# An encoder's second channel mixer with its sample tokens as 2x2 block products, seven for eight

## The chip, the cores and the metric

The kernel runs on one core of one Trainium2 chip. The metric is the time of one execution on the device, in microseconds (us). Of every kernel the median of several executions is given, beside one profiled execution that a hardware profiler recorded.

## The reference

A two-layer encoder over 256 prompt tokens and 1024 sample tokens of width 1024. Layer 0 mixes tokens with a recurrence, layer 1 with a neighbourhood attention; a channel mixer follows each. Only the second channel mixer (layer 1, behind the attention) is at stake here:

```python
D_MODEL = 1024; SEQ = 256; DEC_SEQ = 1024; D_FF = 4 * D_MODEL

def _sq_relu_mlp(h, w_up, w_down):
    return jnp.square(jax.nn.relu(h @ w_up)) @ w_down
...
    x = x + y                                # y: the token mixer, its output product (w_no) in it
    x = x + _sq_relu_mlp(_rms_norm(x, p['norm_mlp_g'][layer]), p['w_up'][layer], p['w_down'][layer])
```

All of it is float32.

## The kernel before

Every array lies with its channels over the 128 partitions, eight blocks of channels deep, and its tokens along the free axis. Tokens go in three segments, `SEGS = [(0,256),(256,768),(768,1280)]`: the prompt (s = 0) and two halves of the sample (s = 1, 2). A float32 product is made of three matmuls on a split of both factors into a rounded part (hi) and what is left (lo): hi by hi, hi by lo, lo by hi. That is `mm3`, lines 108 to 110, one matmul on each line, and these lines are the matmuls of the profile's rows. A weight block is loaded (L101, SyncE's queue), rounded by ScalarE (`whi`, L102), and its rest is subtracted by GpSimd, in the `w_no` part by VectorE (`wlo`, L103). Below, a *unit* is one matmul of 128x128 weights with 512 tokens; one with 256 tokens counts half.

`channel_layer(1, x_d, "at_d", "w_no", out)` does layer 1's mixer, all products being plain:

- *Output product of the attention.* For eight row blocks m of `w_no`, segments 0 and 1, then again for segment 2: `dense` (8 x 3 matmuls), VectorE adds the residual (L1433), ScalarE and GpSimd the squares for the norm (L1260, L1261), and `split_x` writes hi and lo of the scaled x into the tiles `act` (ahp/alp, ahs/als; L1268, L1269).
- *Up and down, interleaved.* For each of 32 hidden blocks f: `up(f, s)` multiplies by `w_up`, takes the ReLU on ScalarE (L1459), the square on GpSimd (L1460), hi on ScalarE (L1462) and lo on VectorE (L1463), into SBUF. `down([f - 1], s)` multiplies the hidden block before it by eight blocks of `w_down`, and VectorE adds each result to x in SBUF (L1481).
- *The norm* is not applied ahead of the products: x is multiplied by the mean square `ms` (`scale`, L1443 to L1446), and at the last hidden block the sum is multiplied by its inverse (L1483) and stored.

```python
            for f in range(2, NF - 1):
                for s in range(3):
                    up(f, s)
                    down([f - 1], s)
                ...
                wdown(f)
```

Each engine works through its queue in the order in which its instructions stand there; a scheduler (Tile) fixes that order when the kernel is built, by its own costs, except where the code pins it for TensorE (`manual_schedule`). Between engines there are semaphores: an instruction that waits holds up all that stand behind it on its engine. Tiles come from pools; a tile that takes over the place of another waits until that one's last reader is done.

## Time and profile before

| | |
|---|---|
| median of 3 executions | 4020.34 us (4017.2 to 4024.3) |
| the profiled execution | 4024.14 us, its span 4022.4 us, mean granted TensorE clock 0.969 |
| TensorE busy | 3744.8 us (93% of the span) |
| VectorE, ScalarE, GpSimd busy | 2477.0, 1535.1, 1501.4 us |
| DMA | 387.74 MB, mean 96 GB/s |

How to read the rows shown below: L108 is a line of the kernel; engines are PE (TensorE matmul), PEld (its weight loads), DVE (VectorE), ACT (ScalarE), POOL (GpSimd), SP (SyncE, which issues transfers). A group's row has its line, engine, operation, `out<-in`, the tile's partitions x elements and the count, then busy us in all, mean ns of one, the engine's idle time just ahead of them and what ended it. Busy engines are not by themselves what bounds: matmuls are pipelined, so that a row's 390 ns for one matmul is a latency, and its price is the distance between two of them.

### The profile page before, as it was taken

How to read it: one execution, taken by the hardware profiler on the slowest of the kernel's cores; microseconds unless marked ns; L12 is line 12 of the kernel's file. 1: busy time of each engine (PE TensorE's matmuls, PEld its weight loads, DVE VectorE, ACT ScalarE, POOL GpSimd, SP SyncE). 2: the span in 40 equal slices, each digit the busy share in tenths (PEclk: the TensorE clock that was granted, in tenths of full speed). 3: DMA queues.
4: the chain of work that ended last, by engine and by line, in shares of the span. 5: the costliest groups of instructions: out<-in, count | busy, mean ns of one | idle time of the engine just before them, and what ended most of it. 6: DMA issues, size and time to landing. Idle time of an engine off the chain costs nothing.

```text
span 4022.4 us, 82971 instructions
## 1 busy us (share of the span) xinstructions
PE 3744.8 (93%) x33028; PEld 3104.7 (77%) x33028; DVE 2477.0 (62%) x4691; ACT 1535.1 (38%) x3587; POOL 1501.4 (37%) x1568
## 2 busy tenths in 40 slices
PE   7888989888888799999999989999989999999999
PEld 4665669766667688888888879777758888888887
DVE  7897975577775466555555560666774755555555
ACT  6776763344445331121121142555663221121121
POOL 4451112365666543222222240455552422222222
PEclk8998989899999899999999999999989999999999
DMA  3326666666776421111111135333344111111111
GB/s 107 92 79 233 230 211 184 162 151 163 178 162 173 145 73 37 37 43 37 37 43 37 37 98 168 80 70 83 78 113 135 47 37 37 43 37 37 43 32 63
DMA packets 397428, 387.74 MB, mean 96 GB/s; under 512 B 163792, under 2 KB 318640, under 8 KB 397040
## 3 DMA queue, kind: packets, MB, share of 16 engines
q1 hardware_dynamic: 337328, 292.10, 26.6%
q10 hardware_dynamic: 46704, 61.35, 4.5%
q0 software_dynamic: 13008, 28.99, 2.4%
q8 instruction: 260, 4.26, 0.5%
q14 instruction: 128, 1.05, 0.1%
HBM read 272.30 MB, written 121.24 MB: 98 GB/s over the span
## 4 chain that ended last, share of the span: by engine, by line
PE 62%; DVE 7%; POOL 4%; issue 4%; ACT 3%; DMA 2%; SPq 0%; ACTq 0%; DVEq 0%; POOLq 0%
PE ps L108 17%; PE ps L109 17%; PE ps L110 17%; PE kps L1003 2%; PE op L1934 1%; PE bo L1044 1%; PE ba L1044 1%; PE pt L1876 1%; ACT ll L1013 1%; PE qps L956 1%; PE bu L1044 1%; POOL z_d L1210 1%; DVE zz L1008 1%; PE nst L1671 1%; PE vps L527 1%
## 5 line engine op out<-in xcount | busy, mean ns | idle before, releaser
L1481 DVE TENSOR_TENSOR x<-ps,x 128x256 f32<-128x256 f32 x1488 | 812.5, 594 | 609.4 <-PE ps L110 609.4
L103 POOL TENSOR_TENSOR wlo<-raw,whi 128x1024 fp32r<-128x1024 f32 (+1 forms) x178 | 391.6, 2200 | 849.0 <-ACT whi L102 848.9
L108 PE MATMUL ps<-ahs,whi 128*128 128x512 f32 x1536 | 612.9, 399 | 0.0
L109 PE MATMUL ps<-als,whi 128*128 128x512 f32 x1536 | 599.5, 390 | 0.4 <-POOL als L1367 0.4
L110 PE MATMUL ps<-ahs,wlo 128*128 128x512 f32 x1536 | 599.1, 390 | 0.0
L108 PE MATMUL ps<-hh,whi 128*128 128x512 f32 (+1 forms) x1536 | 545.5, 355 | 12.2 <-DVE x L1481 12.1
L109 PE MATMUL ps<-hl,whi 128*128 128x512 f32 (+1 forms) x1536 | 544.0, 354 | 0.0
L110 PE MATMUL ps<-hh,wlo 128*128 128x512 f32 (+1 forms) x1536 | 543.6, 354 | 0.0
L102 ACT CAST whi<-raw 128x1024 fp32r<-128x1024 f32 (+1 forms) x206 | 201.2, 977 | 688.9 <-PE ps L109 631.7
L1460 POOL TENSOR_TENSOR rl<-rl 128x512 f32<-128x512 f32 (+1 forms) x192 | 174.1, 907 | 490.3 <-PE ps L110 451.0
L108 PEld LDWEIGHTS ps<-ahs,whi 128*128 128x128 f32 x1536 | 288.9, 188 | 62.2 <-issue 6.9
L110 PEld LDWEIGHTS ps<-ahs,wlo 128*128 128x128 f32 x1536 | 288.5, 188 | 61.8
L108 PEld LDWEIGHTS ps<-hh,whi 128*128 128x128 f32 x1536 | 290.0, 189 | 55.8 <-DVE x L1481 15.6
L109 PEld LDWEIGHTS ps<-als,whi 128*128 128x128 f32 x1536 | 288.9, 188 | 54.0 <-issue 1.0
L110 PEld LDWEIGHTS ps<-hh,wlo 128*128 128x128 f32 x1536 | 290.4, 189 | 40.6
L109 PEld LDWEIGHTS ps<-hl,whi 128*128 128x128 f32 x1536 | 290.4, 189 | 40.1
L1459 ACT ACTIVATE rl<-ps 128x512 f32<-128x512 f32 (+1 forms) x192 | 100.7, 524 | 533.2 <-PE ps L110 533.2
L1462 ACT CAST hh<-rl 128x512 fp32r<-128x512 f32 (+1 forms) x192 | 105.5, 550 | 321.4 <-POOL rl L1460 321.3
L108 PE MATMUL ps<-ahp,whi 128*128 128x256 f32 x768 | 222.1, 289 | 0.0
L1008 DVE TENSOR_TENSOR zz<-kps,cst 128x512 f32<-128x512 f32 x160 | 110.7, 692 | 174.6 <-ACT ll L1013 174.4
L110 PE MATMUL ps<-ahp,wlo 128*128 128x256 f32 x768 | 215.3, 280 | 0.7 <-POOL wlo L103 0.7
L109 PE MATMUL ps<-alp,whi 128*128 128x256 f32 x768 | 215.1, 280 | 0.0
(336 smaller groups left out, 8325.9 us busy)
## 6 DMA issues: line engine op xcount, KB each, us to landing
x<-x_d SPq DMA_DIRECT2D x88, 512.0 KB, 6.3
raw<-in_w_down_dram SPq DMA_DIRECT2D x64, 512.0 KB, 3.5
raw<-in_w_up_dram SPq DMA_DIRECT2D x64, 512.0 KB, 3.5
x_d<-ar ACTq DMA_DIRECT2D x32, 512.0 KB, 3.2
x_d<-bk ACTq DMA_DIRECT2D x32, 512.0 KB, 5.3
bs<-tab SPq DMA_DIRECT2D x128, 96.0 KB, 4.3
v_d<-vt ACTq DMA_DIRECT2D x80, 128.0 KB, 3.5
uv<-v_d SPq DMA_DIRECT2D x80, 128.0 KB, 7.4
```

What stands on the lines that cost most here:

```text
L102: nc.scalar.copy(hi[:, cs], raw)
L103: lo_eng.tensor_tensor(out=lo[:, cs], in0=raw, in1=hi[:, cs].bitcast(F32), op=ALU.subtract)
L108: mm(ps, sh, mh, start=first, stop=False)
L109: mm(ps, sh, ml, start=False, stop=False)
L110: mm(ps, sl, mh, start=False, stop=last)
L1003: mm(J["kp"][out, e, 192 * c + 192 - w:192 * c + 192], x[es, b, 2 * pr + c], x[es, 5 - w // 64:5, 2 * pr + c], start=True, stop=True)
L1008: nc.vector.tensor_tensor(out=z, in0=src[:, :, :, :P], in1=self.mask[d].unsqueeze(1).unsqueeze(1).to_broadcast([P, 2, 2, P]), op=ALU.mult)
L1044: mm = lambda out, a, b, start, stop: nc.tensor.matmul(out, a, b, start=start, stop=stop, skip_group_check=True)
L1459: nc.scalar.activation(r[:, :n], ps[:, :n], AF.Relu)
L1460: nc.gpsimd.tensor_tensor(out=r[:, :n], in0=r[:, :n], in1=r[:, :n], op=ALU.mult)
L1462: nc.scalar.copy(hh[:, :n], r[:, :n])
L1481: nc.vector.tensor_tensor(out=xv, in0=ps[:, :n], in1=xv, op=ALU.add)
```

## The change

`run` calls `mixer7(1, x_d, "w_no", out)` in place of `channel_layer(1, ...)`; layer 0 stays with `channel_layer`, and `act_tiles` only gives its tiles names by which their places can be taken over later. The two halves of the sample make the columns of a 2x2 block matrix B, two halves of the inner dimension its rows; two row blocks of the weight by those halves make A. Winograd's form then needs seven products in place of eight (A11B11, A12B21, S1T1, S2T2, S3T3, S4B22, A22T4), with S sums of weight blocks and T sums of B. The prompt's tokens are done plainly, 256 at a time. There are two stages in place of the interleaving:

- *Up*, 16 steps n, each a pair of hidden blocks. The S of step n + 1 are four GpSimd operations (`up_raw`) on the two loaded weight tiles `raws[0]`, `raws[1]` into `raws[2]`, `raws[3]`; each of the four is then split on ScalarE and VectorE (`up_unit`). Two products that are added accumulate in the same PSUM bank, whose value in between ScalarE copies out (`t1`, `t5`). For n below 14 the seven hidden operands of the down stage (B11, B21, B22, T1 to T4 of the hidden blocks) are formed on GpSimd, split, and stored by SP to DRAM (`h_d`, 512 KB each, through a ring of three tiles `ho`), as are the prompt's two (`hp_d`); step 14 stores its four plain blocks, and step 15 keeps them in SBUF (`keep`).
- *Down*, 16 steps. First pair 15, plain, from SBUF: prompts, then `keep[1]` and `keep[2]`, then `keep[0]` and `keep[3]`. Then pairs 0 to 13 with seven products, four times j each (27 units), and pair 14 plain. Their operands come back from DRAM (`fetch`, on GpSimd's queue, into 13 tiles). VectorE adds PSUM to the accumulators `acc`, 128x1024 at a time, 16 times a step. `down_sums` (GpSimd, 4 x 128x512) and `chunk` (16 casts on ScalarE, 16 subtracts of 128x256 on GpSimd a step) prepare the weights of the next step. The residual, stored to DRAM in the output product (`xn_d`), is loaded, scaled and added by GpSimd over steps 2 to 13; `combine(j)`, 7 GpSimd operations each, makes the four output blocks of the seven sums in step 14, and the last step adds pair 14, scales and stores.

```diff
...
-            return [[pool.tile([P, n], F32R, name=f"{x}{part}{k}") for x in ("ah", "al")] for k in range(KT)]
+            return [[pool.tile([P, n], F32R, name=f"{x}{part}{k}", tag=f"{x}{part}{k}") for x in ("ah", "al")] for k in range(KT)]
...
+    def mixer7(self, layer, x_src, wname, dst):
...
+        xn_d = self.dram("xn_d", [8, P, T])
+        h_d = self.dram("h_d", [NP - 1, 7, P, 2, 512])
+        hp_d = self.dram("hp_d", [NP - 1, 2, P, 2, TP])
...
+        def cut(x, hi, lo, eng):
+            nc.scalar.copy(hi, x)
+            sub(eng, lo, x, hi.bitcast(F32))
...
+            raws = [wr.tile([P, 1024], F32, name="raw", tag=f"raw{i}") for i in range(4)]
...
+            def up_raw(n):
+                r, q = raws[:2], raws[2:]
+                for i in range(2):
+                    nc.sync.dma_start(r[i], a["w_up"][layer, 2 * n + i])
+                add(nc.gpsimd, h0(q[0]), h0(r[1]), h1(r[1]))
+                sub(nc.gpsimd, h1(q[0]), h0(r[0]), h0(r[1]))
+                sub(nc.gpsimd, h0(q[1]), h0(q[0]), h0(r[0]))
+                sub(nc.gpsimd, h1(q[1]), h1(r[0]), h0(q[1]))
...
+            def up_prep(i, n):
+                if i == 0:
+                    up_raw(n)
+                    up_unit(raws[0], ("A11", "A12"))
+                elif i == 1:
+                    up_unit(raws[3], ("S2", "S4"))
+                elif i == 2:
+                    up_unit(raws[2], ("S1", "S3"))
+                else:
+                    up_unit(raws[1], ("A21", "A22"))
...
+            def give(n, i, t):
+                if n == NP - 1:
+                    cut(t, *keep[i], nc.vector)
+                    return
+                o = out_tile()
+                cut(t, o[:, 0], o[:, 1], nc.vector)
+                nc.sync.dma_start(h_d[n, i], o.bitcast(F32))
...
+                for n in range(NP):
+                    nxt = lambda i: up_prep(i, n + 1) if n < NP - 1 else None
+                    plain = n >= NP - 2
+                    b1 = bank()
+                    product(b1, "A11", "B11", True, False)
+                    t1 = tmp("p")
+                    nc.scalar.copy(t1, b1)
+                    ps = bank()
+                    prompt(ps, 0)
+                    give_prompt(n, 0, ps)
+                    product(b1, "A12", "B21", False, True)
+                    h11 = tmp("h")
+                    relu2(h11, b1)
+                    nxt(0)
+                    b6 = bank()
+                    product(b6, "S2", "T2")
+                    add(nc.vector, t1, b6, t1)
+                    give(n, 0, h11)
+                    b5 = bank()
+                    product(b5, "S1", "T1", True, False)
+                    t5 = tmp("q")
+                    nc.scalar.copy(t5, b5)
+                    ps = bank()
+                    prompt(ps, 1)
+                    give_prompt(n, 1, ps)
+                    product(b5, "S4", "B22", False, True)
+                    h12 = tmp("r")
+                    add(nc.vector, h12, b5, t1)
+                    nxt(1)
+                    relu2(h12, h12)
+                    b7 = bank()
+                    product(b7, "S3", "T3")
+                    u3 = tmp("U")
+                    add(nc.vector, u3, b7, t1)
+                    add(nc.gpsimd, t5, u3, t5)
+                    relu2(t5, t5)
+                    nxt(2)
+                    if plain:
+                        give(n, 1, h12)
+                    else:
+                        sub(nc.gpsimd, h12, h12, h11)
+                        give(n, 6, h12)
+                    give(n, 2, t5)
+                    if not plain:
+                        t2 = tmp("T")
+                        sub(nc.gpsimd, t2, t5, h12)
+                        give(n, 4, t2)
+                        sub(nc.gpsimd, h11, t2, h11)
+                        give(n, 5, h11)
+                    b4 = bank()
+                    product(b4, "A22", "T4")
+                    sub(nc.vector, u3, u3, b4)
+                    relu2(u3, u3)
+                    nxt(3)
+                    give(n, 3, u3)
+                    if not plain:
+                        sub(nc.gpsimd, u3, t2, u3)
+                        give(n, 1, u3)
...
+                def chunk(r, n, j, plain):
+                    hi, lo = (z.rearrange("p (o c) -> p o c", o=8) for z in slot())
+                    for t, raw in enumerate(r if plain else (*r, *raws[2:])):
+                        src = raw.rearrange("p (h c) -> p h c", h=2)[:, :, j * P:(j + 1) * P]
+                        os = slice(2 * t, 2 * t + 2)
+                        cut(src, hi[:, os], lo[:, os], nc.gpsimd)
...
+                seq = [NP - 1, *range(NP - 1)]
...
+                for j in range(4):
+                    ps = banks()
+                    plain_sample(ps, n, j, [keep[0], keep[3]])
+                    nc.scalar.copy(acc[j][1][:, 0], ps[:, 0])
+                    nc.scalar.activation(acc[j][1][:, 1], ps[:, 1], AF.Copy, scale=-1.0)
+                    if j == 0:
+                        down_load(rr[0], seq[1])
+                        down_sums(rr[0])
+                    chunk(rr[0], seq[1], j, False)
...
+                hpool = pool("m7h", "left")
+                hr = [hpool.tile([P, 2, 512], F32R, name="h", tag=f"h{i}") for i in range(12)]
...
+                names = ["B11", "p", "B21", "T4", "T2", "B22", "T3", "T1"]
...
+                def fetch():
+                    if cnt[0] < len(want):
+                        n, b = want[cnt[0]]
...
+                                nc.gpsimd.dma_start(v[:, f], hp_d[n, f].bitcast(F32R))
+                            H[n, b] = [pair(v[:, f]) for f in range(2)]
+                        else:
+                            nc.gpsimd.dma_start(t, h_d[n, stored[b]].bitcast(F32R))
+                            H[n, b] = pair(t)
+                for _ in hr:
+                    fetch()
...
+                mid = {2 + 3 * j + part: (j, part) for j in range(4) for part in range(3)}
+                for k in range(1, NP):
...
+                    if k + 1 < NP:
+                        down_load(rr[k % 2], seq[k + 1])
+                        if k + 1 < NP - 1:
+                            down_sums(rr[k % 2])
+                    for j in range(4):
...
+                        def done(b):
+                            if j == 3:
+                                fetch()
+                        if not last:
+                            for i, (ops) in enumerate(((("A11", "B11"), ("p", "p")), (("A12", "B21"), ("A22", "T4")), (("S2", "T2"), ("S4", "B22")), (("S3", "T3"), ("S1", "T1")))):
+                                ps = banks()
+                                for q, (o, b) in enumerate(ops):
+                                    if o == "p":
+                                        plain_prompt(ps[:, 1], n, j, use(b))
+                                    else:
+                                        mm3(ps[:, q], c[o], use(b), True, True)
+                                    done(b)
+                                add(nc.vector, acc[j][i], acc[j][i], ps)
+                            if k + 1 < NP:
+                                chunk(rr[k % 2], seq[k + 1], j, k + 1 == NP - 1)
+                            if j == 3 and k in mid:
+                                residual(*mid[k])
...
-            self.channel_layer(1, x_d, "at_d", "w_no", out)
+            self.mixer7(1, x_d, "w_no", out)
...
```

GpSimd's queue before, in the middle of the interleaving (rl is the hidden block, wlo the weight's rest):

```order
L103 TENSOR_TENSOR wlo_40364<-raw_40365,whi_40363 128x1024 [waits DMAHW5_49,PE_49,Activation_49]
L1460 TENSOR_TENSOR rl_40172<-rl_40172 128x256 [waits Activation_49]
L1460 TENSOR_TENSOR rl_40244<-rl_40244 128x512 [waits Activation_49]
L103 TENSOR_TENSOR wlo_40598<-raw_40599,whi_40597 128x1024 [waits DMAHW4_49,PE_49,Activation_49]
L1460 TENSOR_TENSOR rl_40316<-rl_40316 128x512 [waits Activation_49]
L103 TENSOR_TENSOR wlo_40592<-raw_40593,whi_40591 128x1024 [waits DMAHW7_49,PE_49,Activation_49]
L1460 TENSOR_TENSOR rl_40400<-rl_40400 128x256 [waits Activation_49]
L1460 TENSOR_TENSOR rl_40472<-rl_40472 128x512 [waits Activation_49]
```

GpSimd's queue now, one step of the up stage; its seven hidden operands and the weight sums of the step after the next take turns (tr, tq, th, tU, tT are the temporaries h12, t5, h11, u3 and t2, raw_35258 to raw_35261 the four weight tiles):

```order
L1549 TENSOR_TENSOR tr_37265<-tr_37265,th_37177 128x512 [waits Activation_49]
L1552 TENSOR_TENSOR tq_37219<-tU_37284,tq_37219 128x512 [waits DVE_49]
L1549 TENSOR_TENSOR tT_37300<-tq_37219,tr_37265 128x512 [waits Activation_49,Pool_49]
L1549 TENSOR_TENSOR th_37177<-tT_37300,th_37177 128x512 [waits Pool_49]
L1552 TENSOR_TENSOR raw_35260<-raw_35259 128x512 [waits DMAHW2_49,DVE_49]
L1549 TENSOR_TENSOR raw_35260<-raw_35258,raw_35259 128x512 [waits DMAHW4_49]
L1549 TENSOR_TENSOR raw_35261<-raw_35260,raw_35258 128x512 [waits Pool_49]
L1549 TENSOR_TENSOR raw_35261<-raw_35258,raw_35261 128x512 [waits Pool_49]
L1549 TENSOR_TENSOR tU_37284<-tT_37300,tU_37284 128x512 [waits DVE_49]
```

The subtracts and squares of before are gone, and the four sums on raw stand between the last two operands, T3 (th) and T4 (tU).

ScalarE's queue before, in the same loop:

```order
L1462 CAST hh_40247<-rl_40244 128x512 [waits Pool_49]
L102 CAST whi_40597<-raw_40599 128x1024 [waits DMAHW4_49,PE_49]
L1459 ACTIVATE rl_40316<-ps_40291 128x512 [waits DVE_49,PE_49]
L1462 CAST hh_40319<-rl_40316 128x512 [waits Pool_49]
L102 CAST whi_40591<-raw_40593 128x1024 [waits DMAHW7_49,PE_49]
L1459 ACTIVATE rl_40400<-ps_40375 128x256 [waits DVE_49,PE_49]
L1462 CAST hh_40403<-rl_40400 128x256 [waits Pool_49]
```

ScalarE's queue now, at the same place of the up stage, from the copy of `t1` to that of `t5`:

```order
L1763 COPY tp_37351<-ps_37338 128x512 [waits PE_49]
L1555 CAST ho_37307<-th_37177 128x512 [waits DMAHW1_49,Pool_49]
L1555 CAST ho_37329<-tU_37284 128x512 [waits DMAHW3_49,DVE_49,Activation_49]
L1555 CAST whi_35252<-raw_35258 128x1024 [waits DMAHW4_49,PE_49]
L1555 CAST ho_37334<-tU_37284 128x512 [waits DMAHW4_49,Pool_49]
L1730 ACTIVATE tT_37378<-ps_37353 128x256
L1730 ACTIVATE th_37397<-ps_37338 128x512 [waits DVE_49,PE_49]
L1731 ACTIVATE tT_37378<-tT_37378 128x256 [waits Activation_49]
L1731 ACTIVATE th_37397<-th_37397 128x512 [waits Activation_49]
L1555 CAST ho_37381<-tT_37378 128x256 [waits DMAHW5_49,Activation_49]
L1555 CAST ho_37422<-th_37397 128x512 [waits DMAHW6_49,DVE_49,Activation_49]
L1778 COPY tq_37439<-ps_37426 128x512 [waits PE_49]
```

The copies of t1 and t5 (first and last row) enclose the second cast of tU (T4), which waits for the last of the GpSimd rows above; PE's second product into ps_37426 waits for this copy.

GpSimd's queue now, at the end of pair 15, where the first operands are fetched (the others follow in one run behind these rows):

```order
L1549 TENSOR_TENSOR wlo_35257<-raw_35258,whi_35253 128x256 [waits PE_49,Activation_49]
L1549 TENSOR_TENSOR wlo_35257<-raw_35259,whi_35253 128x256 [waits PE_49,Activation_49]
L1549 TENSOR_TENSOR wlo_35254<-raw_35258,whi_35250 128x256 [waits PE_49,Activation_49]
L1549 TENSOR_TENSOR wlo_35254<-raw_35259,whi_35250 128x256 [waits PE_49,Activation_49]
L1549 TENSOR_TENSOR wlo_35255<-raw_35258,whi_35251 128x256 [waits PE_49,Activation_49]
L1916 DMA h_39967<-h_d_35245 128x1024 [waits DVE_49]
L1549 TENSOR_TENSOR wlo_35255<-raw_35259,whi_35251 128x256 [waits PE_49,Activation_49]
L1913 DMA h_39968<-hp_d_35246 128x2x256 [waits DVE_49]
L1913 DMA h_39968<-hp_d_35246 128x2x256
```

All first fetches but one stand behind the weight subtracts of the third set of pair 15.

GpSimd's queue now, in a seven-product step of the down stage (xt is the residual, h_399xx the ring of operands, raw_39982 and raw_39983 the second pair of weight tiles):

```order
L1929 TENSOR_TENSOR xt_39984<-xt_39984,ms2_35264 128x1024 [waits DMAHW4_49,Pool_49]
L1549 TENSOR_TENSOR wlo_35254<-raw_35259,whi_35250 128x256 [waits PE_49,Activation_49]
L1549 TENSOR_TENSOR xt_39984<-xt_39984 128x512 [waits Pool_49]
L1549 TENSOR_TENSOR wlo_35254<-raw_35261,whi_35250 128x256 [waits PE_49,Activation_49]
L1549 TENSOR_TENSOR wlo_35254<-raw_35260,whi_35250 128x256 [waits PE_49,Activation_49]
L1916 DMA h_39975<-h_d_35245 128x1024 [waits DMASW3_49,PE_49]
L1916 DMA h_39976<-h_d_35245 128x1024 [waits DMASW4_49,PE_49]
L1916 DMA h_39977<-h_d_35245 128x1024 [waits DMASW5_49,PE_49]
L1916 DMA h_39978<-h_d_35245 128x1024 [waits DMASW6_49,PE_49]
L1913 DMA h_39985<-hp_d_35246 128x2x256 [waits DMASW7_49,PE_49]
L1913 DMA h_39985<-hp_d_35246 128x2x256 [waits DMASW0_49]
```

Fetches, weight subtracts, sums and the residual share this one queue.

286 lines of the change are left out of this document (added).

## Prediction

> **What bounds the kernel now.** I read the page's second part, then the stretches of the second channel mixer, then the chain of waits inside it, and then the groups of instructions in that time. The page's slices are 100 us each; the last nine are this mixer:
>
> ```profile
> PE   7888989888888799999999989999989999999999
> ...
> POOL 4451112365666543222222240455552422222222
> PEclk8998989899999899999999999999989999999999
> ```
>
> PE is full and GpSimd at a quarter. The mixer's own stretches (output product, its end, the interleaving of up and down, the end); columns are busy us (instructions) of PE, PEld, DVE, ACT, POOL, then granted clock, DMA share and GB/s:
>
> ```profile
> 3019.00:3125.00 106.00, 106.00 (x567) 91.37 (x568) 43.34 (x62) 37.19 (x56) 31.69 (x21) 1.00 0.41 134
> 3125.00:3190.00 65.00, 60.36 (x311) 50.80 (x310) 57.84 (x74) 17.19 (x29) 39.03 (x26) 0.97 0.13 41
> 3190.00:3970.00 780.00, 780.00 (x4092) 672.44 (x4091) 416.01 (x766) 148.24 (x227) 209.05 (x142) 1.00 0.12 37
> ```
>
> For 780 us PE has no gap. The chain there is matmuls alone, and places one hidden block apart give the price of a unit:
>
> ```profile
> by line: PE ps L109 33.7%; PE ps L108 33.4%; PE ps L110 33.4%
> ...
> 3213.56 0.23 PE ps L109
> ...
> 3240.95 0.23 PE ps L109
> ...
> 3268.33 0.24 PE ps L109
> ```
>
> A hidden block is 60 units up and 60 down: 27.38 us / 120 = 0.228 us a unit. So the matmuls bound this part, and every unit saved counts as long as nothing else becomes late.
>
> **The matmuls.** Before: 480 units (output product) + 32 x 60 + 32 x 60 = 4320. After: 480; up 16 steps of 7 x 12 + 24 (prompt) = 108, that is 1728; down 14 steps of 108 and two plain ones of 120, 1752; together 3960. 360 units fewer: **-82.2 us**. A step of 108 units takes PE 24.65 us. That is certain; what is not is whether the other engines keep 24.65 us a step in their new order. Their prices:
>
> ```profile
> L103 POOL TENSOR_TENSOR wlo<-raw,whi 128x1024 fp32r<-128x1024 f32 x64 | 155.8, 2435 | 365.6 <-ACT whi L102 365.5
> L102 ACT CAST whi<-raw 128x1024 fp32r<-128x1024 f32 x78 | 82.1, 1053 | 308.9 <-PE ps L109 296.9 <-DMA raw<-in_w_no_dram 7.0 <-issue 4.6
> L1462 ACT CAST hh<-rl 128x512 fp32r<-128x512 f32 x64 | 39.8, 621 | 132.8 <-POOL rl L1460 132.8
> L1459 ACT ACTIVATE rl<-ps 128x512 f32<-128x512 f32 x64 | 38.0, 594 | 213.7 <-PE ps L110 213.7
> L103 DVE TENSOR_TENSOR wlo<-raw,whi 128x1024 fp32r<-128x1024 f32 x14 | 17.1, 1223 | 1.9 <-ACT whi L102 1.9
> L1462 ACT CAST hh<-rl 128x256 fp32r<-128x256 f32 x32 | 13.0, 407 | 27.6 <-POOL rl L1460 27.6
> L1459 ACT ACTIVATE rl<-ps 128x256 f32<-128x256 f32 x32 | 12.3, 384 | 58.7 <-PE ps L110 58.7
> ...
> raw<-in_w_up_dram SPq DMA_DIRECT2D x64, 512.0 KB, 3.5
> ...
> raw<-in_w_no_dram SPq DMA_DIRECT2D x14, 512.0 KB, 4.7
> ```
>
> GpSimd's two-input operation on 128x512 is 2435 / 2 = 1.22 us. And VectorE and GpSimd hinder each other when both read two tiles of SBUF, alone and beside one another:
>
> ```profile
> 3149.22 1.75 POOL L1446 TENSOR_TENSOR x<-x,ms 128x512 f32<-128x512 f32 x1
> 3149.95 1.57 DVE L1463 TENSOR_TENSOR hl<-rl,hh 128x512 fp32r<-128x512 f32 x1
> 3303.39 0.69 DVE L1463 TENSOR_TENSOR hl<-rl,hh 128x512 fp32r<-128x512 f32 x1 [0.35 <-ACT hh L1462]
> ```
>
> **The up stage, steps 1 to 14.** A chain runs from one step to the next. Let 0 be the end of A22T4, PE's last product of a step. Its end frees the weight tile into which ScalarE casts raw_35259, A21 and A22 of the next step: behind an operation under way (0.6) and with 1.05 of its own it ends at 1.6. VectorE's rest of it takes 1.22, but GpSimd's T2 subtract holds it up to about 2.5: 3.7. Only then may SP load the block of the step after into raw_35259, 3.5: 7.2. GpSimd's queue now waits for this load, and behind the four sums stands T4's subtract. The sums are 4 x 1.22 and, as an estimate, 0.3 of waiting for each other, 5.2; VectorE's rests of the hidden operands and of a weight (0.69 + 1.22) get between: 14.3. T4's subtract: 15.6. ScalarE's queue waits for this with T4's cast, and behind it are ReLU, square and cast of the first prompt tile and of h11, until the copy of t5: 0.62 + 0.38 + 0.59 + 0.41 + 0.62 + 0.41 + 0.62 + 0.59 = 4.2, less about 0.5, as successive ones overlap: 19.3. PE's S4B22 accumulates in the bank that this copy reads, and is due after 72 units, 16.4. PE waits 2.9 us a step. From below, with no hindrance between VectorE and GpSimd, the copy ends at 16.5: 0.1. From above, with the 4.7 us landing in place of 3.5: 4.1. I take 2.9, since the 3.5 has 64 loads behind it and the rests are two-input operations like the row of 1.57: 14 x 2.9 = **+40.6** (1 to 57).
>
> [...]
>
> Other waits of this stage are met: A12B21 needs the copy of t1, out at about 4.8 us, and is due after 24 units, 5.5. ScalarE's work is four weight casts, seven of 128x512, two of 128x256, two copies, and ReLU and square four times in full and twice in half width: 4.2 + 4.3 + 0.8 + 1.2 + 4.9 + 1.6 = 17 us of 24.65; seven of eight banks are in use. The stores, nine a step on SP, 4 MB with the weights' 1 MB against 24.65 us, are 200 GB/s; the output product has moved twice that for some us:
>
> ```profile
> GB/s 3 73 308 36 406 252 395 60 128 420 215 150 81 174 233 130 22 245 114 24 245 118 18 173 0 24 167 0 0 0 189 188 28 173 12 179 25 168 13 177
> ```
>
> The sums of x for T2 to T4 (VectorE, GpSimd) fall into the end of the output product, where PE was idle 4.6 us before (65.00 - 60.36, scaling of x); that scaling goes: 0, between -4.6 and +5.
>
> **Up to down.** GpSimd's last t5 add of step 15 stands behind `down_sums` of pair 0, which wait for a load of w_down into tiles that pair 15's weights have to leave first: `keep[2]` is ready at about 9.8 us after the up stage (load 3.5, sums 5.2 and the add), and its first user, behind the prompts and 27 units, is due at 6.2: **+3.6** (0 to 5).
>
> **The first fetches.** They stand on GpSimd behind the weight subtracts of pair 15's third set, which wait for its last products. The nearest transfers into or from DRAM take
>
> ```profile
> L101 POOL DMA_DIRECT2D raw<-in_w_nq_dram x14 | 8.2, 587 | 4.2 <-POOL wlo L103 4.2
> ...
> x_d<-ar ACTq DMA_DIRECT2D x32, 512.0 KB, 3.2
> ...
> at_d<-ot POOLq DMA_DIRECT2D x14, 256.0 KB, 3.6
> ```
>
> Each has 0.59 us of issue and 3.2 to 4.7 us to land, so the first operand comes about 5 us after pair 15's last product, and eight of 512 KB follow at 1.3 us each (400 GB/s, the best slices above) while the first group uses them within 6.2 us: **+9** (5 to 14).
>
> **The down stage.** GpSimd has per step 16 weight subtracts of 128x256, four sums and nine issues. The subtract is 2.435 / 4 = 0.61 or, by the row below, 0.74; I take 0.69.
>
> ```profile
> L1261 POOL TENSOR_TENSOR ms<-ms,sq 128x256 f32<-128x256 f32 x14 | 10.3, 739 | 14.3 <-ACT sq L1260 14.3
> ...
> 2354.46 2.54 POOL L1483 TENSOR_TENSOR x<-x,ms 128x512 f32<-128x512 f32 x2
> ```
>
> 11.0 + 5.2 + 9 x 0.6 = 21.6 us. The residual adds in 12 of the 14 steps, per block row j, 2.5 + 2 x 1.22 (first half), 2.5 + 3 x 1.22 (second), 1.27 + 1.22 (prompt): 13.6 in three steps, 4.6 on average. 26.2 against PE's 24.65: GpSimd becomes the bound by 1.6 us a step, and there is no cover, since fetches and weights of the next step stand in the same queue. 12 x 1.6 = **+19**. Below: 0.61 for the subtracts gives 24.5, so nothing a step but a late last fetch (it may start only when the last group's product is done, lands 4.5 us later, and is wanted 4.1 us into the next step), some 0.6: +7. Above: 0.74 and sums at 1.3, 27.1: +31.
> VectorE keeps up: it adds 128x1024 from PSUM 16 times, and six of half that took
>
> ```profile
> 3304.00 3.67 DVE L1481 TENSOR_TENSOR x<-ps,x 128x512 f32<-128x512 f32 x6
> ```
>
> so 16 x 2 x 0.61 = 19.5 of 24.65.
>
> **Clock and tail.** A gap of PE has cost clock in this mixer:
>
> ```profile
> 3159.64 0.58 PE L108 MATMUL ps<-hh,whi 128*128 128x256 f32 x1 [3.33 <-DVE x L1481]
> ...
> 3160.00:3170.00 10.00, 10.00 (x39) 7.87 (x39) 9.82 (x18) 0.47 (x1) 1.25 (x2) 0.87 0.15 48
> ```
>
> After 3.33 us of idling the next 10 us had 0.87, so 1.3 us lost. The two gaps between the stages: **+3** (0 to 4). At the end VectorE scaled and added one tile behind PE:
>
> ```profile
> 4014.06 0.24 PE ps L110
> ...
> 4014.32 0.70 DVE x L1481
> ...
> 4015.05 0.69 DVE x L1483
> ```
>
> Before, 2.8 us to the last scaling's end; now the last row of blocks has a sample add and two products of 512 and a prompt's left, about 6.5: **+3.7** (0 to 6).
>
> **The sum.** -82.2 + 40.6 + 3.6 + 9 + 19 + 3 + 3.7 = -3.3. The profiled execution took 4024.1 (span 4022.4 and 1.7 around it), so 4020.8; it lies 3.8 above the median of the three, so **4017**. All bounds in favour: -82.2 + 1 + 0 + 5 + 7 + 0 + 0 - 4.6 = -74; all against: -82.2 + 57 + 5 + 14 + 31 + 4 + 6 + 5 = +40.
>
> **The rivals.**
> *The up chain hides.* If GpSimd's sums run beside VectorE's subtracts without loss, the copy of t5 ends at 16.5 and PE never waits there: -3.3 - 39 = -42, so 3978. For it: one end of my bound, and sums that read one tile (the first does). Against it: the row of 1.57 us.
> *The clock falls in every up step.* The chain's wait is 2.9 us, just short of the 3.33 which cost 1.3 us. If loads land in 4.7 us, as they did beside x's loads in the output product, the wait is 4.1; with the clock 14 x (1.2 + 1.3) = +35: 4052, slower. It decides from a landing of about 3.9 us on. For it: nine stores a step on the same queue as the load. Against it: DMA is at half of what it has done.
> [...]
> *Late loads without the clock.* 14 x 1.2 = +17: 4034.
>
> **How the numbers follow.** The forecast, a saving that the waits nearly eat up, 0.5, itself from -30 to +25 by the fetches and GpSimd's pace; the hidden chain 0.22; clock 0.17; late loads 0.11. The three executions differ by 7 us, so a change under 0.2%, 8 us, can't be told from none. Faster: the hidden chain and 0.18 of the forecast, 0.40. Same: 0.19 of the forecast. Slower: both other rivals and 0.13, 0.41. The range goes from the hidden chain's 3978 a little down to 3974, and from 4052 up to 4064, for GpSimd's pace on top.
>
> **What would show it.** In the up stage: a gap of about 2.9 us ahead of the second product into each S1T1 bank, ended by ScalarE, and the last GpSimd sum ending near 14 us after A22T4; no gap there, and the first term is wrong. At the down stage's start: a gap of 5 to 14 us ended by a transfer. In its steps 2 to 13: GpSimd at over 90%, and PE's gaps ended by GpSimd or by its fetches, 1 to 2 us a step; with GpSimd at 80% and no gaps, the pace is mis-sized. PE's work itself must be 360 units shorter. I am wrong altogether if a wait that I count as met (t1's copy, ho's ring of three stores) ends late in every step.

## The result, and the profile after

The changed kernel takes 4050.4 us (median of 4, 4044.8 to 4055.5) against 4020.8 (4 runs): ratio 1.0073, 95% interval 1.0054 to 1.0093. That is slower by 0.7%, where the forecast 4017 was a little faster than before; it lies inside the forecast's range. The profiled execution has a span of 4053.0 us (before 4022.4): 30.6 more.

The page of the changed kernel, in the same rows as the page of before (slices of 101 us; the mixer is the last ten):

```profile
PE   7888989888888899999999989999979999989998
...
POOL 5451112365566542222222241455454554459996
PEclk8998989999999899999999999999989999989999
```

Stretches of it (columns as before: PE, PEld, DVE, ACT, POOL busy, granted clock, DMA share, GB/s): output product, first two up steps, the other up steps, the last one's end, pair 15, seven-product steps up to a gap that ends at 3911 us, the rest of them, the last step. Steps of the down stage are counted with pair 15 as step 0, so that pair 0 is step 1 and the last step 15:

```profile
3019.00:3131.80 112.80, 109.79 (x575) 93.98 (x574) 58.49 (x80) 46.27 (x71) 42.30 (x29) 1.00 0.46 153
3131.80:3206.00 74.20, 63.10 (x316) 52.47 (x315) 55.03 (x56) 41.63 (x70) 35.39 (x24) 0.95 0.33 122
3206.00:3550.00 344.00, 319.60 (x1679) 273.98 (x1678) 209.86 (x216) 196.44 (x342) 173.47 (x114) 1.00 0.52 196
3550.00:3574.10 24.10, 24.10 (x131) 20.84 (x130) 6.90 (x10) 13.36 (x28) 13.79 (x23) 1.00 0.33 110
3574.10:3614.70 40.60, 30.10 (x144) 25.64 (x142) 8.68 (x12) 14.89 (x33) 23.56 (x25) 0.87 0.15 52
3614.70:3911.00 296.30, 275.92 (x1414) 232.12 (x1414) 206.09 (x170) 68.91 (x174) 270.06 (x343) 0.98 0.65 216
3911.00:4017.00 106.00, 100.62 (x494) 85.96 (x494) 82.96 (x67) 17.72 (x45) 94.59 (x110) 0.94 0.45 147
4017.00:4053.00 36.00, 18.36 (x87) 15.50 (x85) 32.49 (x31) 0.00 (x0) 9.58 (x9) 0.78 0.39 146
```

PE, which had no gap in 780 us before, now idles in every stage but one, and the clock falls behind the longer gaps (0.87 in pair 15, 0.78 in the last step). The gaps one by one:

*Up.* The predicted chain is there. The timeline's rows give start, duration in us, and in brackets the idle time ahead and what ended it. In order: the load, the four sums, T4's subtract, T4's cast, the copy of t5, PE's second product into its bank:

```profile
3335.86 0.33 SPq L1684 DMA_DIRECT2D raw<-in_w_up_dram  x1
...
3339.41 1.29 POOL L1552 TENSOR_TENSOR raw<-raw 128x512 f32<-128x512 f32 x1 [2.42 <-DMA raw<-in_w_up_dram]
3340.65 5.22 POOL L1549 TENSOR_TENSOR raw<-raw 128x512 f32<-128x512 f32 x3
...
3345.83 1.28 POOL L1549 TENSOR_TENSOR tU<-tT,tU 128x512 f32<-128x512 f32 x1
...
3347.15 0.62 ACT L1555 CAST ho<-tU 128x512 fp32r<-128x512 f32 x1 [4.68 <-POOL tU L1549]
...
3350.07 0.59 ACT L1778 COPY tq<-ps 128x512 f32<-128x512 f32 x1
...
3350.71 0.50 PE L1546 MATMUL ps<-ahs,whi 128*128 128x512 f32 x1 [1.69 <-ACT tq L1778]
```

All gaps of the steps from 3190 us on, as one group:

```profile
L1546 PE MATMUL ps<-ahs,whi 128*128 128x512 f32 x212 | 84.7, 400 | 24.4 <-ACT tq L1778 24.4
```

*Start of pair 15.* 9.7 us. GpSimd's t5 addition is late; behind it stands VectorE's last subtract of the up stage, behind that the copy of the first prompt product, and PE waits for this copy, since the second prompt product shares its PSUM tile:

```profile
3580.01 1.26 POOL L1552 TENSOR_TENSOR tq<-tU,tq 128x512 f32<-128x512 f32 x1
...
3581.30 0.69 DVE L1549 TENSOR_TENSOR tU<-tU,ps 128x512 f32<-128x512 f32 x1 [4.42 <-POOL tq L1552]
...
3584.47 0.68 DVE L1877 COPY acc<-pd 128x512 f32<-128x512 f32 x1
...
3585.21 0.79 PE L1546 MATMUL pd<-ho,whi 128*128 128x256 f32 x2 [9.71 <-DVE acc L1877]
```

*Seven-product steps.* Groups of that stage: PE's gaps by fetches and by VectorE's additions, and GpSimd's issues:

```profile
L1546 PE MATMUL pd<-h,whi 128*128 128x512 f32 x848 | 270.3, 401 | 24.6 <-DMA h<-h_d 16.6 <-DVE acc L1552 7.8
...
L1916 POOL DMA_DIRECT2D h<-h_d x101 | 54.8, 552 | 16.2 <-PE pd L1546 10.2 <-DMA h<-h_d 2.5 <-DMA h<-hp_d 2.3
```

5.6 us of the 16.6 lie ahead of pair 0 and 0.7 inside its step; the other gaps by fetches come in steps 3, 4, 6, 7, 8, 10 and 11. GpSimd is busy for 270.06 of 296.3 us.

*Steps 11 to 13* (the expectation on the inverses, which counts pair 15 as the first step, calls them 12 to 14). Three gaps that I had not forecast, of 2.4, 3.2 and 2.1 us, the second of them:

```profile
3936.90 2.38 POOL L1929 TENSOR_TENSOR xt<-xt,ms 128x1024 f32<-128x1024 f32 x1
...
3939.31 1.76 DVE L1986 RECIPROCAL ms<-ms 128x128 f32<-128x128 f32 x2 [5.21 <-POOL xt L1929]
...
3940.99 2.29 DVE L1552 TENSOR_TENSOR acc<-acc,pd 128x1024 f32<-128x1024 f32 x2
...
3942.30 1.19 PE L1546 MATMUL pd<-h,whi 128*128 128x512 f32 x2 [3.24 <-DVE acc L1552]
```

The reciprocal overwrites ms, which GpSimd still has to read; VectorE's additions queue behind it until PE has no free bank.

*Last step.* One scaling of 128x1024 took 18.32 us; the three like it that follow took 1.23 each. Meanwhile GpSimd worked without a pause, on combine operations but for two weight subtracts:

```profile
4009.34 18.32 DVE L1993 TENSOR_TENSOR acc<-acc,ms 128x1024 f32<-128x1024 f32 x1
...
4018.02 7.34 POOL L1552 TENSOR_TENSOR acc<-acc 128x512 f32<-128x512 f32 x6
4025.33 1.25 POOL L1549 TENSOR_TENSOR acc<-acc 128x512 f32<-128x512 f32 x1
...
4028.91 0.79 PE L1546 MATMUL pd<-h,whi 128*128 128x256 f32 x2 [11.30 <-DVE acc L1552]
```

### The profile page after: what moved, and what is told of

Its sections match the earlier page's. It is cut to its first block, busy times and chain, and to the rows that moved or that the text cites. A ratio compares the mean times of both kernels' runs of the same rounds, so it can differ in the third digit from the quotient of the medians.

```text
span 4053.0 us, 83598 instructions
## 1 busy us (share of the span) xinstructions
PE 3693.9 (91%) x32668; PEld 3053.4 (75%) x32668; DVE 2592.9 (64%) x4380; ACT 1725.7 (43%) x4029; POOL 1866.8 (46%) x2035
## 5 line engine op out<-in xcount | busy, mean ns | idle before, releaser
L1481 DVE TENSOR_TENSOR x<-ps,x 128x256 f32<-128x256 f32 (+1 forms) x744 | 406.2, 594 | 302.8 <-PE ps L110 302.8
L1546 PE MATMUL pd<-h,whi 128*128 128x512 f32 (+1 forms) x1328 | 361.8, 362 | 37.1 <-DVE acc L1552 19.1
L108 PE MATMUL ps<-ahs,whi 128*128 128x512 f32 x896 | 362.5, 405 | 0.0
L1552 DVE TENSOR_TENSOR acc<-acc,pd 128x1024 f32<-128x1024 f32 x240 | 284.6, 1192 | 108.2 <-PE pd L1546 96.1
L109 PE MATMUL ps<-als,whi 128*128 128x512 f32 x896 | 349.8, 390 | 0.9 <-POOL als L1367 0.9
L110 PE MATMUL ps<-ahs,wlo 128*128 128x512 f32 x896 | 349.9, 390 | 0.0
L1546 PEld LDWEIGHTS pd<-h,whi 128*128 128x128 f32 x1328 | 239.8, 196 | 80.6 <-issue 16.6
L108 PE MATMUL ps<-hh,whi 128*128 128x512 f32 (+1 forms) x768 | 272.5, 355 | 9.2 <-DVE x L1481 9.2
L109 PE MATMUL ps<-hl,whi 128*128 128x512 f32 (+1 forms) x768 | 272.0, 354 | 0.0
L110 PE MATMUL ps<-hh,wlo 128*128 128x512 f32 (+1 forms) x768 | 271.9, 354 | 0.0
```

Of the source, the lines that this page charges most:

```text
L108: mm(ps, sh, mh, start=first, stop=False)
L109: mm(ps, sh, ml, start=False, stop=False)
L110: mm(ps, sl, mh, start=False, stop=last)
L1481: nc.vector.tensor_tensor(out=xv, in0=ps[:, :n], in1=xv, op=ALU.add)
L1546: mul(ps, w[wi], b[bi], start=first and i == 0, stop=last and i == 2, skip_group_check=True)
L1552: eng.tensor_tensor(out=out, in0=x, in1=y, op=ALU.add)
```

## The experiments

Executions of one kernel differed by up to 32 us in these runs (the kernel before: 4002 to 4034 in 45 executions over three series), so a single edit is judged by its gaps in the trace, and by the time where it moves more. Part of the difference lies ahead of the mixer, in code that is the same in all: its first matmul came between 3010.9 us (T4 on VectorE) and 3025.1 us (the last step's scaling). The mixer alone, from that matmul to the end of the profiled execution, can be split into PE's gaps (0.05 us and more), the time lost to a lower clock (estimated as half of PE's time at half the clock), and the rest, which is PE's work and the tail:

| us | mixer | gaps | clock | rest |
|---|---|---|---|---|
| before | 1003.5 | 4.6 | 1.7 | 997.2 |
| changed | 1034.4 | 86.1 | 21.0 | 927.3 |
| last step's scaling | 1028.3 | 77.4 | 23.9 | 927.0 |
| inverses | 1035.0 | 80.7 | 26.5 | 927.8 |
| T4 on VectorE | 1027.1 | 82.3 | 15.2 | 929.6 |
| last t5 | 1037.1 | 85.2 | 25.1 | 926.8 |
| PE's order | 1020.8 | 74.7 | 15.9 | 930.2 |
| fetches on SP | 1002.4 | 66.2 | 10.9 | 925.3 |
| first fetches | 1005.7 | 65.9 | 14.7 | 925.1 |
| five edits | 969.8 | 35.2 | 10.0 | 924.6 |
| start of the down stage | 951.1 | 24.2 | 3.4 | 923.6 |
| with T4 on VectorE | 941.2 | 14.8 | 4.9 | 921.6 |
| the same, PE's old order | 962.3 | 34.0 | 5.2 | 923.1 |

The rest is 67 to 76 us below that of before in every version: the work is saved, and gaps and clock decide what is left of it.

**The last step's scaling.** Edit, in the same way for its three kinds of output:

```diff
-                            add(nc.vector, o, o, ps)
-                            nc.vector.tensor_tensor(out=o, in0=o, in1=ms[1]...
+                            add(nc.vector, ps, o, ps)
+                            nc.vector.tensor_tensor(out=o, in0=ps, in1=ms[1]...
```

> The changed kernel, but in the last step (pair 14) VectorE writes the sum of accumulator and product back into PSUM and scales it from there, so that none of these instructions reads two tiles of SBUF; nothing else moves. [...] Then it takes about 1.2 us, the 11.3 us gap of TensorE behind it and some 3 us of lower clock go: 4034 to 4039 us, against 4050. Theory B: it waited for data from GpSimd (the combining of the sums): the same wait then stands at another instruction, and the time stays within 3 us of 4050.

Measured: 4049.5 us (4035.7 to 4055.2). The groups of the scaling from 3990 us to the end, of the changed kernel and of this one:

```profile
L1993 DVE TENSOR_TENSOR acc<-acc,ms 128x1024 f32<-128x1024 f32 x4 | 22.0, 5498 | 0.1
```
```profile
L1993 DVE TENSOR_TENSOR acc<-pd,ms 128x1024 f32<-128x1024 f32 x4 | 4.9, 1225 | 0.1
```

The 11.3 us gap is gone; from the first to the last prompt product of the last step it is 20.7 us in place of 34.5: 13.8 less, near the 11.3 and some 3 expected. GpSimd's combining ran on without a pause until 4041.4 us, past the first three of these scalings, so theory B is out. The time of the whole doesn't show it, and missed the 4034 to 4039: in this execution the mixer began 6.4 us later, and three up steps lost clock, in the profiled one of the changed kernel one.

**The inverses.** Edit: `reciprocal(out=inv[s]...)` into tiles of their own, used by the last scalings.

> The changed kernel, but the ten reciprocals of the mean square write into tiles of their own in place of overwriting it. Theory A: the gaps of 2.4, 3.2 and 2.1 us near the end of steps 12 to 14 come from a reciprocal that may overwrite only when GpSimd's scaling of the residual has read, with VectorE's additions queued behind it; they go, with 6 to 7 us of lower clock: 4035 to 4039 us. Theory B: VectorE is simply full there (19.5 us of additions and up to 9.4 us of reciprocals in a step of 24.9): the gaps stay about as long in one step, and the time is 4046 to 4053.

Measured: 4051.4 us (4040.7 to 4056.0), so the time missed theory A. The three gaps of 2.4, 3.2 and 2.1 us are gone from the trace, as theory A has it; the last step's gap grew from 11.3 to 13.1, and six of 13 up steps lost clock where one had. From the start of pair 0 to the end it took 429.6 us in place of 438.2.

**T4 on VectorE.** Edit:

```diff
-                        sub(nc.gpsimd, u3, t2, u3)
+                        sub(nc.vector, u3, t2, u3)
```

> The changed kernel, but the subtract that makes operand T4 runs on VectorE, so that it doesn't stand behind the four weight sums in GpSimd's queue. Theory A (the chain of the prediction, load to sums to T4 to ScalarE's casts to the copy of t5): the copy ends some 3 us earlier, the gaps of 1.6 to 2.0 us in 13 up steps (24 us in all) close: 4024 to 4031 us. Theory B: ScalarE is held by the ring of three operand tiles (its cast of B21 waited 3.3 us for a store): the gaps stay above 1 us, 4043 to 4053.

Measured: 4047.1 us (4032.8 to 4061.5); the gaps as a group:

```profile
L1546 PE MATMUL ps<-ahs,whi 128*128 128x512 f32 x216 | 86.2, 399 | 19.1 <-ACT tp L1763 14.9 <-ACT tq L1778 4.2
```

The chain through the sums was real: the copy of t5 no longer ends late in most steps. But A12B21 now waits for the copy of t1, up to 1.5 us a step. The wait that I counted as met was met only because PE came late. Neither theory; of 24.4 us of gaps, 5.3 were won.

**The last t5.** Edit: in step 15 alone, `add(nc.vector, t5, u3, t5)`.

> The changed kernel, but the addition that makes t5 in step 15 alone runs on VectorE, so that it doesn't stand behind the weight sums of pair 0 in GpSimd's queue. Theory A: the 9.7 us gap at the start of the down stage comes from that one addition; it shrinks below 1.5 us, with 2 to 3 us of lower clock: 4037 to 4042 us. Theory B: the weights of pair 15 or the kept operands are late by themselves: a gap of 4 to 8 us stays there, 4044 to 4049.

Measured: 4060.0 us (4050.2 to 4061.7), more than the changed kernel; the gap shrank from 9.7 to 8.1 only, and five up steps lost clock. A gap of this size is theory B's, the time neither theory's. In the trace, VectorE's addition now stands behind a rest whose cast on ScalarE stands behind casts of pair 0's weights, and these wait for the same sums.

**PE's order.** Edit: S2T2 ahead of A12B21, S3T3 ahead of S4B22.

> The changed kernel, but TensorE's order in the up stage puts S2T2 ahead of A12B21 and S3T3 ahead of S4B22, so that the copies of t1 and t5 each have 12 units (2.7 us) more before a product must accumulate into their bank. Nothing is taken away from any engine. Theory A (each wait is a fixed chain that ends 1.6 to 2 us after TensorE's place): all 13 gaps close, 24 us, and the 5.4 us gap of step 0 shrinks to about 2.7: 4015 to 4025 us. Theory B (the engines behind are full over a whole step, so that a wait only moves, as it moved to the copy of t1 when T4 went to VectorE): gaps above 1 us a step stay at other places, 4035 to 4050.

Measured: 4041.9 us (4034.9 to 4053.9). Eleven gaps of 1.0 to 2.2 us stay (14.4 in all), at the copy of t5 again: theory B. Two waits of ScalarE ahead of its casts could still be the cause, for T4 behind GpSimd's sums and for a store to leave the ring of three operand tiles:

```profile
L1555 ACT CAST ho<-tU 128x512 fp32r<-128x512 f32 x24 | 14.9, 621 | 58.6 <-POOL tU L1549 44.4 <-DMA h_d<-ho 12.5 <-DVE tp L1552 1.7
```

Which of them it is, this run doesn't show; T4 on VectorE in this order, below, does. The products for the norm now wait 7.6 us for their tile of ones, in place of 4.6.

**The fetches.** Edit, for both kinds of operand:

```diff
-                            nc.gpsimd.dma_start(t, h_d[n, stored[b]].bitcast(F32R))
+                            nc.sync.dma_start(t.bitcast(F32), h_d[n, stored[b]])
```

> The changed kernel, but the operands of the down stage are fetched by SP's queue in place of GpSimd's. Theory A (GpSimd's pace: 0.55 to 0.72 us of issue each, in the queue with subtracts and the residual): GpSimd loses 5 us of work a step, the gaps ended by fetches in steps 3 to 13 (about 16 us with the following groups) go, and the first fetches come about 1 us earlier: 4030 to 4038 us. Theory B (the transfers themselves: a burst of 4 MB at some 400 GB/s at the end of each step): the gaps stay, within 5 us of 4050.

Measured: 4026.9 us (12 runs, 4018.5 to 4037.8), ratio to before 1.0016 (1.0004 to 1.0028): the largest gain of a single edit. The seven-product steps (columns as above):

```profile
3617.00:3913.00 296.00, 288.46 (x1516) 247.60 (x1516) 224.94 (x187) 74.44 (x186) 230.24 (x257) 0.99 0.64 235
```

PE's gaps from pair 0 on:

```profile
L1546 PE MATMUL pd<-h,whi 128*128 128x512 f32 x848 | 263.8, 392 | 7.6 <-DMA h<-h_d 6.9 <-ACT whi L1555 0.6
```

GpSimd's busy time falls from 270 to 230 us in 296. The fetch gaps are gone but for those of pair 0 (5.6 us ahead of it and two of 0.4), while a fetch lands hardly sooner (512 KB in 6.6 us, on GpSimd's queue 6.9; 256 KB in 7.9 and 7.0) and the stage moves more, 235 GB/s: GpSimd's pace, not the transfers. The gaps of steps 11 to 13 went too, since GpSimd reads ms earlier: VectorE idles 3.4, 2.1 and 2.5 us ahead of the first reciprocals in place of 5.2, 5.2 and 4.1.

**The first fetches.** Edit: `hr = hr[2:10] + hr[10:12] + hr[:2] + hr[12:]`, on top of the run before.

> As the run before it (fetches by SP's queue), and the ring of 13 tiles begins with those whose places are free from the end of the up stage, in place of the tiles over the kept operands of pair 15. Theory A: the first operands then arrive during pair 15, and the start of pair 0 loses its gaps of 5.6, 1.2 and 0.4 us and 4 us of lower clock: 10 to 12 us less than the run before it. Theory B: SP's queue holds the fetches back behind loads that wait for GpSimd: no difference between the two.

Measured: 4022.4 us (12 runs, 4016.2 to 4034.7), 4.5 less than the run before it, with ranges that overlap; the gap ahead of pair 0 is 5.5 us as before. Theory B: SP's queue has a load of w_down ahead of the fetches, which waits for GpSimd's last weight subtract.

**Five edits together.** The small products for the norm moved behind `give_prompt` of step 1; the inverses, the last scaling, PE's order, and the fetches on SP with the ring in its new order.

> Five edits together: the last step's sums scaled from PSUM, inverses in own tiles, the far copies, the fetches early and on SP, and the three small products for the norm moved behind the first products of step 1 (they waited 4.6 us for a tile of ones). If the gaps are separate causes that add up: 24 (up) + 14 (last step) + 9 (inverses) + 16 (fetches) + 11 (first fetches) + 6 (ones): about 75 to 80 less than 4050, 3970 to 3980 us, 1% below the kernel before. If what one edit frees is taken by the next wait: 4000 to 4020.

Measured: 3996.5 us (3983.7 to 4005.3), ratio to before 0.9941 (0.9919 to 0.9963). Between the two sums: what was local adds up, the up stage keeps 14 us of gaps, and 6.1 and 5.5 us stay around pair 15.

**The start of the down stage.** Edits on top of these five:

```diff
-                    nc.sync.dma_start(r[i], a["w_down"][layer, 2 * n + i])
+                    (nc.sync if n == NP - 1 else nc.gpsimd).dma_start(r[i], a["w_down"][layer, 2 * n + i])
...
-                    if j % 2 == 0:
-                        ps = banks()
+                    ps = banks()
```

> The five edits together, and two more at the start of the down stage: the loads of w_down from pair 0 on are issued by GpSimd's queue, so that the first fetches don't stand behind one of them on SP's, and each of the four prompt products of pair 15 has a PSUM tile of its own. Theory A: the first fetches run during pair 15, and the 5.5 us gap ahead of pair 0 goes with 3 to 4 us of clock; the 6.1 us gap at the start of pair 15 was the sharing of a tile by two products, and shrinks to about 2: 13 less than the five edits alone (3996), 3980 to 3986 us. Theory B: the first gap is the lateness of the kept operand of t5 itself, and only moves to the next set of products: 8 to 9 less.

Measured: 3975.0 us (3969.9 to 3985.9), ratio 0.9879 (0.9863 to 0.9895). No gap ahead of pair 0, and 2.1 us in pair 15: theory A, and 21 us less than the five edits alone in place of 13. In the profiled executions the mixer took 18.7 less: 11.0 in gaps, 6.6 in clock that is no longer lost behind them, and 1.1 of rest.

**T4 on VectorE, again,** on top of that, in the new and in the old order of PE.

> As start_fixed, and T4's subtract on VectorE as well. In the far order the last wait of an up step (1.0 to 1.9 us, 14 in all) ends with T4 and ScalarE's casts behind it. If GpSimd's sums still hold T4: gaps below 0.5 us, 10 to 14 less than start_fixed. If the ring of three operand tiles holds it (ScalarE's casts of T3 and B21 wait 1.7 and 2.4 us for stores there): at most 5 less.

> As start_t4, but in the old order of TensorE in the up stage. With T4 on VectorE the waits there were 0.7 to 1.5 us at the copies of t1 and t5, 18 us in all. If nothing but TensorE's order differs, it lies 3 to 8 us above start_t4, and 2 us either way around start_fixed.

Measured: 3963.0 us (3961.0 to 3972.3), ratio 0.9850 (0.9834 to 0.9867), and 3985.4 us (3975.3 to 3993.2), 0.9900 (0.9883 to 0.9916). In the new order GpSimd's sums were what held T4: the up steps keep four gaps below 1 us, 2.5 in all. ScalarE waits for the ring as long as it did (12.7 us against 12.5 ahead of T4's and B21's casts), so it was not the ring that held PE:

```profile
L1555 ACT CAST ho<-tU 128x512 fp32r<-128x512 f32 x26 | 16.2, 621 | 54.0 <-DVE tU L1549 41.3 <-DMA h_d<-ho 12.7
```

The old order costs 22 us and not 3 to 8: 19 us of it are gaps, nearly all at the copies of t1 and t5. The two edits, which alone won 5 and 10 of the 24.4 us of gaps, need each other: T4 on VectorE takes the wait off t5, the new order off t1. The steps of up and down in the new order, the fastest version:

```profile
3187.00:3530.00 343.00, 340.50 (x1812) 292.99 (x1811) 246.41 (x246) 212.47 (x372) 169.26 (x107) 1.00 0.57 208
3590.00:3893.00 303.00, 303.00 (x1611) 262.05 (x1610) 237.68 (x196) 76.77 (x195) 263.82 (x301) 1.00 0.62 224
```

## Why the prediction was wrong

Against the span of before, each stage of the changed kernel less its units at 0.228 us (gaps and lost clock in it), beside the term of the sum. What the kernel before lost itself is taken off in the rows of the start and of the tail; 24.88 us is what each of four down steps without a gap took, and why it isn't 24.65 stays open:

| | predicted | measured |
|---|---|---|
| 360 units fewer | -82.2 | -82.2 |
| a step without gaps is 24.88 us, not 24.65 | 0 | +9 |
| start of the up stage | 0 | +9 |
| up, chain of steps | +40.6 | +27 |
| pair 15, clock in it | +5 | +13 |
| first fetches, clock behind | +10.5 | +11 |
| fetches in the steps | +19 | +16 |
| steps 11 to 13 | 0 | +14.5 |
| last step and tail | +3.7 | +13.5 |
| sum | -3.3 | +31 |

The matmuls saved were certain and came. The sum failed because waits that it put at nothing, or too low, add up to more than the saving; that the up chain was put 13.6 us too high hid as much of it, and that the measured time lies inside the range is luck to that extent.

- *The up chain was right in its links and too large by half.* The load was issued 3.3 us after A22T4's end (3.7 in the working), the sums took 6.5 us (7.1; the subtracts among them 1.60 us each, 1.28 in the down stage), T4 and ScalarE 4.8 (5.0). Each was a little long, and a wait is the small difference of long sums: 1.7 for 2.9. That the chain is alone in setting it was wrong, as T4 on VectorE showed.
- *The start of the up stage* got two gaps that I had set against the one before (4.6): A12B21 of step 0 waits 5.4 us for the first copy of t1, and the norm's products 4.6 for a tile of ones, which GpSimd fills late.
- *Up to down.* The late t5 was right, its victim not: PE was to wait for `keep[2]` behind 27 units, and waited at the second prompt product, with 6 of them done. I had followed GpSimd's queue but not VectorE's, in which the prompt's copy stands behind that subtract, nor that two products share a tile.
- *GpSimd's pace and the first fetches were right*, in cause and nearly in size: over steps 2 to 10 GpSimd's work is 25.4 us a step (26.2 in the working), and the steps 26.6. The fetches on SP show the first; the start of the down stage, where they run during pair 15, the second.
- *"VectorE keeps up" is the step that failed.* I counted its 16 additions a step and not what else stands in its queue: ten reciprocals with a wait on GpSimd, 14.5 us with the clock behind it. The inverses in tiles of their own show the cause: these gaps, 7.8 us, go, and with them the clock lost behind them.
- *The tail, +3.7 with a bound of 6, is the other.* Only the lengths were added up; it took 13.5. L1993 reads two tiles of SBUF, as the row of 1.57 us did on which the up stage's wait rests, and the first scaling runs into GpSimd's combining: it took 18.32 us, and 1.22 us from PSUM. By what it is held up no run shows.
- *Clock.* I priced the two gaps between the stages, +3. It was lost behind ten places in the profiled execution, 21.0 us in all against 1.7 before, and so lies in nearly every row of the table. The 10 us after the gaps of 5.55, 3.24 and 11.30 us:

```profile
3620.00:3630.00 10.00, 8.44 (x27) 6.21 (x27) 2.49 (x3) 1.09 (x3) 5.49 (x9) 0.62 1.20 403
...
3942.00:3952.00 10.00, 9.70 (x36) 8.34 (x37) 8.74 (x10) 1.62 (x4) 6.29 (x11) 0.67 0.59 155
...
4028.00:4038.00 10.00, 9.09 (x36) 7.85 (x37) 9.90 (x15) 0.00 (x0) 0.00 (x0) 0.71 0.62 236
```

- *The rivals.* The hidden chain didn't come. The clock rival, at 4052, came to the right time by luck: in the profiled execution the steady up steps kept their clock. In those of the variants up to five of 13 steps lost it, at gaps of 1.7 to 2.1 us, and that is part of why executions differ. Nor were loads late: the median landing of a w_up block in this stage is 3.5 us, the longest 3.9.

## What to carry to other kernels

Before counting a saving on the engine that bounds, write down for every other engine all that stands in its queue in that stage, one-off work too (reciprocals, scalings, loads for the next stage), and ask of each what it waits for; here waits, most of them from the order in a queue, and the clock behind them cost more than the saved products. A wait that is met may be met only because another wait is not: two edits that closed 5 and 10 us of gaps alone closed 22 together, on top of the other edits. And beside GpSimd's combining, which ran without a pause, one operand in PSUM brought VectorE's scaling from 18.32 us to 1.22.

## What the runs showed of the hardware

- The first scaling of the last step, with both inputs in SBUF, took 18.32 us in the changed kernel, behind the GpSimd operation under way and 14 more; it ended 1.1 us after GpSimd's last one. With the inverses in their own tiles it took 20.14 us. With the sum in PSUM it took 1.22 us, with GpSimd combining beside it as before.
- The clock fell behind some short gaps. Over the gaps of 0.4 us and more at the copies of t1 and t5, from the third up step on, in the twelve profiled executions of the changed kernel and its variants: behind none of 97 gaps up to 1.73 us, 16 of 47 between 1.74 and 2.2 us, five of six above 2.8 us. Where it fell, the granted clock over the next 6 us was 0.50 to 0.76.
- Two equal gaps didn't cost the same. In the mixer of the changed kernel the clock stood at 0.50 for 3.41 us six times, for 6.83 us once, for 10.24 us twice, for 13.65 us once, and from 4050.9 us to the end. A gap of 2.0 us ending at 3412.06, in the run with the last scaling from PSUM, lies inside the first of these rows; over the second, 3.41 us, the clock is 0.50, and about 1.7 us are lost:

```profile
3410.11:3413.53 3.42, 1.47 (x6) 1.24 (x7) 1.69 (x4) 3.00 (x8) 0.00 (x0) 1.00 0.70 271
3413.53:3416.94 3.41, 3.41 (x9) 2.63 (x8) 0.76 (x2) 1.00 (x1) 0.00 (x0) 0.50 0.56 215
```

Of a gap of 2.0 us ending at 3431.01, in the changed kernel, 0.7 us lie in the first row and 1.3 us in the second, and nothing is lost:

```profile
3426.26:3429.67 3.41, 2.72 (x24) 2.51 (x22) 1.29 (x2) 2.23 (x6) 1.15 (x1) 1.00 0.80 279
3429.67:3433.09 3.42, 2.08 (x9) 1.74 (x10) 1.54 (x3) 2.39 (x6) 0.00 (x0) 1.00 0.79 310
3433.09:3436.50 3.41, 3.41 (x17) 2.83 (x16) 1.92 (x2) 2.22 (x3) 0.34 (x1) 1.00 0.39 142
```

What decides between the two, this pair alone doesn't show.
